# Output and MLP down-projection in weight blocks of 512 rows by 512 columns instead of 1024 by 256

## The chip, the cores and the metric

The kernel runs on one core of one Trainium2 chip. The metric is device time in microseconds of one execution; before the change it is the median of three runs.

## The reference

A two-layer hybrid backbone works on 256 context tokens and 256 latent tokens of width 1024, all in float32. In each layer three parallel mixers read one input projection, their branches are projected and merged by sigmoid gates, and one output projection follows. Then comes a squared-ReLU MLP. Both results are normalised, scaled by a gate and added to the residual stream. In the second layer only the latent tokens are needed.

```python
def merge_branches(ys, gates, w_branch, w_out):
    g = jax.nn.sigmoid(gates.reshape(gates.shape[:2] + (N_BRANCHES, D_MODEL)))
    merged = g[..., 0, :] * (ys[0] @ w_branch[0])
    for j in range(1, N_BRANCHES):
        merged = merged + g[..., j, :] * (ys[j] @ w_branch[j])
    return merged @ w_out

def sq_relu_mlp(h, w_up, w_down):
    return jnp.square(jax.nn.relu(h @ w_up)) @ w_down
...
        x = x + m_l[2] * rms_norm(y_l, norm_g[l, 1])
        h_l = modulate(rms_norm(x, norm_g[l, 2]), m_l[3], m_l[4])
        x = x + m_l[5] * rms_norm(sq_relu_mlp(h_l, w_mlp_up[l], w_mlp_down[l]), norm_g[l, 3])
```

The two products that the change touches are `merged @ w_out` (1024 by 1024) and `... @ w_down` (4096 by 1024).

## The kernel before

**Numbers in two parts.** Every float32 operand of a large product is split into a high part (rounded to the matmul's reduced format) and a low part (what is left). A product is summed from three matmuls: high by high, high by low and low by high. `weights` (L196) loads a block of 128 x 2048 values in two transfers into one of five `raw` slots, then makes the high part by four casts of 128 x 512 on ScalarE (L226) and the low part by four subtractions on VectorE (L227). Two such blocks fit into `whl`, so that one is converted while the other is used. `wblock` (L232) names the rows and columns of the weight that go into a block.

**Two forms of product.** `mm_cm` (L241) holds 128 x 128 of the weight stationary and moves up to 512 tokens; its matmuls are on L248 to L250. `mm_tm` (L252) holds 128 tokens of the activation stationary and moves columns of the weight, so that the result has tokens on the partitions; its matmuls are on L260 to L262. Each result is summed in one of eight PSUM banks of 512 float32 columns. From the output projection on, `dps` deals four of them out in turn, as b_84 to b_87 in the names below.

**The stage of the change.** `tm_out` (L636) computes the output projection and the MLP's down-projection with `mm_tm`. The tokens are four row tiles of 128: 0 and 1 the context, 2 and 3 the latents; layer 1 has only 2 and 3. A block is 1024 rows (eight steps of 128) by 256 columns, so the output's 1024 columns take four blocks. For each block and each row tile 8 x 3 matmuls of 256 columns are summed in half a bank. The tile is then taken out:

```python
if add:
    nc.vector.tensor_tensor(out=o, in0=src, in1=o, op=ALU.add)
    src = o
elif not gains:
    nc.scalar.copy(o, src)
if gains:
    nc.scalar.activation(junk[:, 0:256], src, AF.Square, scale=D ** -0.5, accum_out=yss[tt][:, b:b + 1])
    nc.vector.tensor_tensor(out=o, in0=src, in1=gains(tt)[:, b * 256:b * 256 + 256], op=ALU.mult)
```

The MLP's hidden width of 4096 is done in four quarters (`qd`): an up-projection of 1024 columns (`cm_blocks`), then `tm_out` over these 1024 rows of `w_down`. Quarter 0 copies the sum out (L655), quarters 1 to 3 add to it (L652), and in quarter 3, as in the output projection, the sum of squares (L657) and the multiply by the gain (L659) follow. `seqs` lists which row tiles share which block: in layer 0's quarters 0 to 2 all four tiles share each block; in its quarter 3 and its output projection the blocks are loaded once for tiles 0 and 1 and again for 2 and 3; in layer 1 tiles 2 and 3 share each block, and the last two blocks are held together, so that tile 2 is done before tile 3.

**What follows a finished row tile.** `after` runs `post` (the mean of squares L629, the power -1/2 on GpSimd L454, and the update of the residual L633), then `prenorm` (Square L566, the sum L568, L454, scaling on VectorE L573 and ScalarE L575, eight transposes on TensorE L581) and `modulate` (scale and shift L598 on VectorE and L596 on ScalarE, high part L603, low part L605), which writes the next stage's activations `h`. After the kernel's last product only `post` and the store of the output are left.

**What sets the order.** Each engine executes its instructions in one order that a scheduler fixes at build time from priorities; conversions and what takes tiles out of PSUM have a higher priority (`hp`). In layer 0's MLP VectorE also computes the second layer's modulation vectors (`ada_acc`, L403), a few steps after each weight block.

## Time and profile before

| what | value |
|---|---|
| median of three runs | 1625.68 us (1623.34 to 1628.14) |
| the profiled execution's own time | 1622.66 us |
| its span | 1620.9 us |
| TensorE busy | 1569.2 us (97%) |
| VectorE busy | 1091.5 us (67%) |
| ScalarE busy | 782.5 us (48%) |
| GpSimd busy | 387.8 us (24%) |
| transfers | 220.26 MB, mean 136 GB/s |

The span runs from the first to the last instruction of the profiled execution; the 1.8 us beside it are its start and end. Shares of busy time are means over stages with different limits, and a matmul's busy time overlaps that of the next one, so a stage is read from the starts of its matmuls and from what its engines wait for. PE is TensorE, PEld its weight loads, DVE VectorE, ACT ScalarE, POOL GpSimd and SP the queue of the transfers. L12 is line 12 of the kernel.

### The profile page before, as it was taken

The page shows a single profiled execution, that of the slowest core. Times are in us where ns is not written, and L with a number is a line of the kernel's source. Part 1 is how long each engine was busy: PE and PEld are TensorE (multiplying, and loading weights), DVE is VectorE, ACT ScalarE, POOL GpSimd, SP SyncE. Part 2 cuts the span into 40 slices and gives each one's busy share as a digit, 9 for nine tenths or more (in the row PEclk, how much of TensorE's full clock was granted, in tenths as well). Part 3 has the DMA queues.
Part 4 walks back from the last instruction along what each step waited for, and adds up shares of the span by engine and source line. Part 5 has one row for each costly group of instructions (what it writes and reads, how often), then busy time and mean ns, then how long its engine had stood idle before and what let it go on. Part 6 is the DMA issues. An engine that isn't in the chain of part 4 may idle for free.

```text
span 1620.9 us, 30093 instructions
## 1 busy us (share of the span) xinstructions
PE 1569.2 (97%) x11806; PEld 1401.7 (86%) x11806; DVE 1091.5 (67%) x1994; ACT 782.5 (48%) x1648; POOL 387.8 (24%) x419
## 2 busy tenths in 40 slices
PE   6999999999999999999999999999998999989998
PEld 4788888887777789888898989999897999989998
DVE  4655544676576578687878756776668788765555
ACT  4443433455444457533323146644455656666554
POOL 1142415050510001310102011364455350211001
PEclk9999999999999999999999999999999999989999
DMA  9723243324332346466556534432434254446662
GB/s 282 230 79 118 80 130 117 92 66 130 129 93 53 117 141 195 147 189 188 173 178 195 156 104 133 129 118 73 124 104 105 66 162 113 156 131 182 183 182 92
DMA packets 234270, 220.26 MB, mean 136 GB/s; under 512 B 24400, under 2 KB 226320, under 8 KB 234128
## 3 DMA queue, kind: packets, MB, share of 16 engines
q1 hardware_dynamic: 234128, 218.34, 45.1%
q8 instruction: 92, 1.51, 0.4%
q14 instruction: 50, 0.41, 0.1%
HBM read 217.26 MB, written 1.05 MB: 135 GB/s over the span
## 4 chain that ended last, share of the span: by engine, by line
PE 84%; DVE 4%; POOL 4%; DMA 2%; ACT 2%; issue 2%; SPq 1%; DVEq 0%; POOLq 0%; ACTq 0%
PE b L248 15%; PE b L249 15%; PE b L250 15%; PE b L260 9%; PE b L261 9%; PE b L262 9%; DMA arf<-in_w_ada_dram 1%; POOL arf L906 1%; PE b L364 1%; POOL arf L796 1%; PE b L1109 1%; PE b L936 1%; PE b L1096 1%; DVE whl L227 1%; PE b L937 1%
## 5 line engine op out<-in xcount | busy, mean ns | idle before, releaser
L227 DVE TENSOR_TENSOR whl<-raw,whl 128x512 fp32r<-128x512 f32 x588 | 431.9, 755 | 213.0 <-ACT whl L226 201.0
L226 ACT CAST whl<-raw 128x512 fp32r<-128x512 f32 x588 | 356.1, 619 | 247.5 <-PE b L262 111.8
L248 PE MATMUL b<-h,whl 128*128 128x512 f32 (+1 forms) x1296 | 448.1, 347 | 1.1 <-ACT arf L951 0.6
L250 PE MATMUL b<-h,whl 128*128 128x512 f32 (+1 forms) x1296 | 445.4, 344 | 0.9 <-DVE whl L227 0.8
L249 PE MATMUL b<-h,whl 128*128 128x512 f32 (+1 forms) x1296 | 444.7, 343 | 0.0
L248 PEld LDWEIGHTS b<-h,whl 128*128 128x128 f32 x1296 | 247.7, 191 | 33.4 <-ACT whl L226 2.1
L250 PEld LDWEIGHTS b<-h,whl 128*128 128x128 f32 x1296 | 246.8, 191 | 29.4 <-issue 1.6
L249 PEld LDWEIGHTS b<-h,whl 128*128 128x128 f32 x1296 | 247.1, 191 | 28.1 <-issue 2.4
L262 PE MATMUL b<-whl,arr 128*128 128x256 f32 x768 | 215.9, 284 | 1.9 <-DVE arr L1320 1.9
L261 PE MATMUL b<-whl,arr 128*128 128x256 f32 x768 | 217.5, 284 | 0.0
L260 PE MATMUL b<-whl,arr 128*128 128x256 f32 x768 | 217.5, 284 | 0.0
L1319 POOL TENSOR_TENSOR arf<-arf 128x256 f32<-128x256 f32 (+1 forms) x68 | 62.3, 916 | 427.7 <-ACT arr L1318 424.1
L260 PEld LDWEIGHTS b<-whl,arr 128*128 128x128 f32 x768 | 147.5, 192 | 1.4 <-DVE arf L652 0.8
L262 PEld LDWEIGHTS b<-whl,arr 128*128 128x128 f32 x768 | 146.8, 192 | 2.1 <-DVE arr L1320 2.1
L261 PEld LDWEIGHTS b<-whl,arr 128*128 128x128 f32 x768 | 147.5, 192 | 0.1
L260 PE MATMUL b<-whl,h 128*128 128x256 f32 x512 | 146.6, 288 | 0.0
L261 PE MATMUL b<-whl,h 128*128 128x256 f32 x512 | 146.0, 286 | 0.0
L262 PE MATMUL b<-whl,h 128*128 128x256 f32 x512 | 144.7, 285 | 0.0
L906 POOL TENSOR_TENSOR arf<-arf,cst 32x256 f32<-32x256 f32 x104 | 94.3, 907 | 192.7 <-ACT arf L951 71.0
L454 POOL TENSOR_TENSOR sm<-sm,nhalf 128x1 f32<-128x1 f32 (+2 forms) x42 | 33.2, 794 | 345.2 <-DVE sm L629 247.2
L403 DVE SCALAR_TENSOR_TENSOR arf<-arf,CA 128x1024 f32<-128x1024 f32 x84 | 109.3, 1345 | 4.8 <-DMA arf<-in_w_ada_dram 4.8
L260 PEld LDWEIGHTS b<-whl,h 128*128 128x128 f32 x512 | 98.6, 193 | 3.2 <-ACT arf L740 0.8
(224 smaller groups left out, 2504.3 us busy)
## 6 DMA issues: line engine op xcount, KB each, us to landing
raw<-in_w_in_dram SPq DMA_DIRECT2D x110, 512.0 KB, 3.9
arf<-in_w_ada_dram SPq DMA_DIRECT2D x80, 512.0 KB, 4.7
raw<-in_w_mlp_down_dram SPq DMA_DIRECT2D x72, 512.0 KB, 3.7
raw<-in_w_mlp_up_dram SPq DMA_DIRECT2D x64, 512.0 KB, 3.9
raw<-in_w_out_dram SPq DMA_DIRECT2D x24, 512.0 KB, 3.6
arf<-in_w_ada_dram SPq DMA_DIRECT2D x32, 256.0 KB, 5.8
raw<-in_w_branch_dram SPq DMA_DIRECT2D x16, 512.0 KB, 4.2
raw<-in_w_in_dram SPq DMA_DIRECT2D x32, 128.0 KB, 3.3
```

Of the source, the lines that this page charges most:

```text
L226: self.behind(ops, lambda: nc.scalar.copy(r32(h), src))
L227: self.split_op = self.behind(ops, lambda: nc.vector.tensor_tensor(out=r32(l), in0=src, in1=h, op=ALU.subtract))
L248: nc.tensor.matmul(ps, wh, xh[:, t0:t0 + n], start=start and k == 0, stop=False)
L249: nc.tensor.matmul(ps, wh, xl[:, t0:t0 + n], start=False, stop=False)
L250: nc.tensor.matmul(ps, wl, xh[:, t0:t0 + n], start=False, stop=stop and k == nk - 1)
L260: nc.tensor.matmul(ps, xh, wh, start=start and k == 0, stop=False)
L261: nc.tensor.matmul(ps, xh, wl, start=False, stop=False)
L262: nc.tensor.matmul(ps, xl, wh, start=False, stop=stop and k == nk - 1)
L403: self.nc.vector.scalar_tensor_tensor(out=a[:, :], in0=raw[:, :], scalar=ca[:, k, s:s + 1], in1=a[:, :], op0=ALU.mult, op1=ALU.add)
L454: self.nc.gpsimd.tensor_tensor(out=r, in0=ms, in1=self.nhalf[:, 0:cols], op=ALU.pow)
L906: nc.gpsimd.tensor_tensor(out=b[o, 0:LAT], in0=x[i], in1=self.cst[i, C_RS:C_RS + LAT], op=ALU.mult)
L1319: nc.gpsimd.tensor_tensor(out=r[:, c], in0=r[:, c], in1=r[:, c], op=ALU.mult)
```

## The change

A block is now 512 rows (four steps of 128) by 512 columns: the same 2048 columns in `whl`, the same bytes. An output column half takes two blocks, one for the upper and one for the lower 512 rows (`kh` 0 and 1), and a row tile's sum over both fills a whole PSUM bank. `order` takes all row tiles of a group through `kh` 0, each into a bank of its own, then all through `kh` 1, and takes each tile out when its second part is done. In layer 1's last group (`whole`) both blocks are loaded first, and tile 2 is finished before tile 3. The operations that take a tile out work on 512 columns instead of 256, and a row tile has two partial sums of squares instead of four.

```diff
--- before.py
+++ after.py
@@ -135,7 +135,7 @@
         self.oml = const("oml", 8)
         self.nhalf = const("nhalf", 8)
         self.ones = const("ones", 32)
-        self.yss = const("yss", 20)
+        self.yss = const("yss", 12)
         self.sm_t = const("sm", 512)
         self.sm_i = 0
         self.raw = const("raw", RAWS * 1024)
@@ -638,26 +638,38 @@
 
         nc = self.nc
         junk = self.A.get(1)
-        left = {tt: 4 for tt in y}
-        for tts, blocks in seqs:
-            blks = [(b, self.wblock(w, r0, 8, b * 256, 256)) for b in blocks]
-            for tt in tts:
-                for b, blk in blks:
-                    ps = self.dps()
-                    self.mm_tm(ps[:, 0:256], blk, 8, 0, 256, act, tt)
-                    o = y[tt][:, b * 256:b * 256 + 256]
-                    with self.hp():
-                        src = ps[:, 0:256]
-                        if add:
-                            nc.vector.tensor_tensor(out=o, in0=src, in1=o, op=ALU.add)
-                            src = o
-                        elif not gains:
-                            nc.scalar.copy(o, src)
-                        if gains:
-                            nc.scalar.activation(junk[:, 0:256], src, AF.Square, scale=D ** -0.5,
-                                                 accum_out=yss[tt][:, b:b + 1])
-                            nc.vector.tensor_tensor(out=o, in0=src, in1=gains(tt)[:, b * 256:b * 256 + 256], op=ALU.mult)
-                left[tt] -= len(blks)
+        left = {tt: 2 for tt in y}
+
+        def finish(tt, b, ps):
+            o = y[tt][:, b * 512:b * 512 + 512]
+            with self.hp():
+                src = ps
+                if add:
+                    nc.vector.tensor_tensor(out=o, in0=src, in1=o, op=ALU.add)
+                    src = o
+                elif not gains:
+                    nc.scalar.copy(o, src)
+                if gains:
+                    nc.scalar.activation(junk[:, :], src, AF.Square, scale=D ** -0.5, accum_out=yss[tt][:, b:b + 1])
+                    nc.vector.tensor_tensor(out=o, in0=src, in1=gains(tt)[:, b * 512:b * 512 + 512], op=ALU.mult)
+            left[tt] -= 1
+
+        for tts, halves, whole in seqs:
+            for b in halves:
+                ps = {}
+                order = [(kh, tt) for kh in range(2) for tt in tts]
+                blks = {}
+                if whole:
+                    order = [(kh, tt) for tt in tts for kh in range(2)]
+                    blks = {kh: self.wblock(w, r0 + kh * 512, 4, b * 512, 512) for kh in range(2)}
+                for kh, tt in order:
+                    if kh not in blks:
+                        blks[kh] = self.wblock(w, r0 + kh * 512, 4, b * 512, 512)
+                    if not kh:
+                        ps[tt] = self.dps()
+                    self.mm_tm(ps[tt], blks[kh], 4, 0, 512, act, tt, kt0=kh * 4, start=not kh, stop=kh == 1)
+                    if kh:
+                        finish(tt, b, ps[tt])
             for tt in tts:
                 if gains and left[tt] == 0:
                     after(tt)
@@ -1273,10 +1285,10 @@
         sv = self.scale_vecs(l, 1)
         y = {tt: A.get(2) for tt in tts}
         if not last:
-            seqs = [((0, 1), (b,)) for b in range(4)] + [((2, 3), (b,)) for b in range(4)]
+            seqs = [((0, 1), (0, 1), False), ((2, 3), (0, 1), False)]
         else:
-            seqs = [((2, 3), (0,)), ((2, 3), (1,)), ((2, 3), (2, 3))]
-        yss = {tt: self.yss[:, tt * 5:tt * 5 + 5] for tt in tts}
+            seqs = [((2, 3), (0,), False), ((2, 3), (1,), True)]
+        yss = {tt: self.yss[:, tt * 3:tt * 3 + 3] for tt in tts}
 
         late = []
 
@@ -1355,11 +1367,11 @@
                 if not last:
                     sv = self.scale_vecs(l + 1, 0)
             if last and qd == 3:
-                seqs = [((2, 3), (0,)), ((2, 3), (1,)), ((2, 3), (2, 3))]
+                seqs = [((2, 3), (0,), False), ((2, 3), (1,), True)]
             elif qd == 3:
-                seqs = [((0, 1), (b,)) for b in range(4)] + [((2, 3), (b,)) for b in range(4)]
+                seqs = [((0, 1), (0, 1), False), ((2, 3), (0, 1), False)]
             else:
-                seqs = [(tts, (b,)) for b in range(4)]
+                seqs = [(tts, (0, 1), False)]
             self.tm_out(I["w_mlp_down"][l], qd * 1024, act, y, yss, seqs, qd > 0, gains if qd == 3 else None, after)
             for b in ab.values():
                 b.free()
```

TensorE at the start of quarter 0's down-projection in layer 0 (b_85 and b_86 are the banks of row tiles 0 and 1, `arr` holds the activations, `whl` the weights). Before, tile 1's steps with a jump back to tile 0's last step:

```order
L262 MATMUL b_86<-whl,arr 128x256
L260 MATMUL b_86<-whl,arr 128x256
L261 MATMUL b_86<-whl,arr 128x256
L260 MATMUL b_85<-whl,arr 128x256
L261 MATMUL b_85<-whl,arr 128x256
L262 MATMUL b_86<-whl,arr 128x256
```

After, the same place at the step from tile 0 to tile 1:

```order
L260 MATMUL b_85<-whl,arr 128x512
L261 MATMUL b_85<-whl,arr 128x512
L262 MATMUL b_85<-whl,arr 128x512
L260 MATMUL b_86<-whl,arr 128x512
L261 MATMUL b_86<-whl,arr 128x512
```

Before, the schedule leaves tile 0 after 21 of its 24 matmuls, ahead of the step on the eighth activation, and comes back to it; now a tile's run is twelve matmuls on four activations, and the eighth activation is used only after all four tiles have had their first run.

VectorE at the end of layer 1's output projection (b_86 is tile 3's last result, b_88 to b_91 the transposed rows, `sm` and `yss` the sums). Before:

```order
L629 TENSOR_REDUCE sm<-yss 128x1
L659 TENSOR_TENSOR arf<-b_86,arf 128x256
L573 TENSOR_SCALAR arf<-arf,sm 128x512
L633 SCALAR_TENSOR_TENSOR arf<-arf,sm 128x512 x2
L598 TENSOR_SCALAR arf<-b_90,sb,M_67 128x128 x3
L598 TENSOR_SCALAR arf<-b_89,sb,M_67 128x128 x3
L568 TENSOR_SCALAR sm<-sm 128x1
L605 TENSOR_TENSOR h<-arf,h 128x4x128
L573 TENSOR_SCALAR arf<-arf,sm 128x512
L598 TENSOR_SCALAR arf<-b_91,sb,M_67 128x128 x4
L603 CAST h<-arf 128x4x128
L605 TENSOR_TENSOR h<-arf,h 128x4x128 x2
```

After (the multiply of L659 is now on L654):

```order
L629 TENSOR_REDUCE sm<-yss 128x1
L654 TENSOR_TENSOR arf<-b_86,arf 128x512
L633 SCALAR_TENSOR_TENSOR arf<-arf,sm 128x512 x2
L568 TENSOR_SCALAR sm<-sm 128x1 x2
L573 TENSOR_SCALAR arf<-arf,sm 128x512 x2
L598 TENSOR_SCALAR arf<-b_89,sb,M_67 128x128 x3
L598 TENSOR_SCALAR arf<-b_90,sb,M_67 128x128 x3
L598 TENSOR_SCALAR arf<-b_91,sb,M_67 128x128 x4
L603 CAST h<-arf 128x4x128
L605 TENSOR_TENSOR h<-arf,h 128x4x128 x3
```

Tile 2's six L598 and its L605 stood ahead of tile 3's L573; now both tiles' L568 and L573 stand ahead of all ten L598, and three L605 stand at the end.

VectorE at the end of the kernel (b_85 and b_86 were tile 3's last two results, b_86 is now its last). Before:

```order
L652 TENSOR_TENSOR arf<-b_85,arf 128x256
L659 TENSOR_TENSOR arf<-arf 128x256
L652 TENSOR_TENSOR arf<-b_86,arf 128x256
L629 TENSOR_REDUCE sm<-yss 128x1
L659 TENSOR_TENSOR arf<-arf 128x256
L633 SCALAR_TENSOR_TENSOR arf<-arf,sm 128x512 x2
```

After (the add of L652 is now on L648):

```order
L633 SCALAR_TENSOR_TENSOR arf<-arf,sm 128x512 x2
L648 TENSOR_TENSOR arf<-b_86,arf 128x512
L629 TENSOR_REDUCE sm<-yss 128x1
L654 TENSOR_TENSOR arf<-arf 128x512
L633 SCALAR_TENSOR_TENSOR arf<-arf,sm 128x512 x2
```

The order of the last steps is the same; the add and the multiply of the last tile are twice as wide, and there is one pair of them where there were two.

## Rows read from the trace of the kernel before

**Rows 1.** The page: span, TensorE's busy time (PEld its weight loads), chain that ended last.
```profile
span 1620.9 us, 30093 instructions
...
PE 1569.2 (97%) x11806; PEld 1401.7 (86%) x11806; DVE 1091.5 (67%) x1994; ACT 782.5 (48%) x1648; POOL 387.8 (24%) x419
...
PE 84%; DVE 4%; POOL 4%; DMA 2%; ACT 2%; issue 2%; SPq 1%; DVEq 0%; POOLq 0%; ACTq 0%
```

**Rows 2.** Stretches: length, then busy us per engine, granted clock, DMA share, GB/s.
```profile
620.00:640.00 20.00, 20.00 (x171) 20.00 (x170) 18.74 (x42) 18.14 (x47) 4.25 (x6) 1.00 0.62 189
1000.00:1040.00 40.00, 40.00 (x337) 40.00 (x337) 36.45 (x79) 29.71 (x74) 12.96 (x13) 1.00 0.61 181
1440.00:1600.00 160.00, 160.00 (x1336) 160.00 (x1335) 88.80 (x158) 90.98 (x180) 18.12 (x30) 1.00 0.56 170
1422.00:1432.00 10.00, 8.19 (x35) 7.17 (x36) 7.92 (x19) 8.00 (x17) 1.82 (x2) 0.50 0.03 5
```

**Rows 3.** Timeline of TensorE, last down-projection: start us, duration us, line, tiles.
```profile
1599.72 0.28 PE L262 MATMUL b<-whl,arr 128*128 128x256 f32 x1
...
1612.20 0.28 PE L261 MATMUL b<-whl,arr 128*128 128x256 f32 x1
```

**Rows 4.** Timeline of TensorE, a branch projection of layer 0.
```profile
299.65 0.39 PE L248 MATMUL b<-arr,whl 128*128 128x512 f32 x1
...
306.00 0.39 PE L249 MATMUL b<-arr,whl 128*128 128x512 f32 x1
```

**Rows 5.** Groups by line and shape, TensorE: xcount, busy us, mean ns, idle before.
```profile
L261 PE MATMUL b<-whl,arr 128*128 128x256 f32 x768 | 217.5, 284 | 0.0
...
L249 PE MATMUL b<-h,whl 128*128 128x256 f32 x608 | 173.7, 286 | 0.0
...
L260 PE MATMUL b<-whl,h 128*128 128x256 f32 x512 | 146.6, 288 | 0.0
```

**Rows 6.** Waits of TensorE: us in total, times, longest.
```profile
PE b L262 <- DVE arr L1320: 1.9, 1, 1.9
...
PE b L248 <- ACT h L603: 1.5, 1, 1.5
...
PE b L249 <- POOL h L605: 0.7, 1, 0.7
```

**Rows 7.** Groups by line and shape: conversions (L227, L226), eviction L652, multiply L1167.
```profile
L227 DVE TENSOR_TENSOR whl<-raw,whl 128x512 fp32r<-128x512 f32 x588 | 431.9, 755 | 213.0 <-ACT whl L226 201.0 <-PE b L250 3.6 <-PE b L249 2.5
L226 ACT CAST whl<-raw 128x512 fp32r<-128x512 f32 x588 | 356.1, 619 | 247.5 <-PE b L262 111.8 <-PE b L249 82.9 <-issue 13.7
...
L652 DVE TENSOR_TENSOR arf<-b,arf 128x256 f32<-128x256 f32 x72 | 30.0, 422 | 29.3 <-PE b L262 27.9
...
L1167 DVE TENSOR_TENSOR arf<-b,arf 128x512 f32<-128x512 f32 x24 | 16.5, 690 | 20.6 <-PE b L250 20.5
```

**Rows 8.** Timeline, layer 1, end of the output projection to the MLP's first matmul.
```profile
1421.05 2.00 DVE L598 TENSOR_SCALAR arf<-b,sb,M 128x128 f32<-128x128 f32 x6
...
1423.96 0.48 DVE L573 TENSOR_SCALAR arf<-arf,sm 128x512 f32<-128x512 f32 x1
...
1425.73 1.37 DVE L598 TENSOR_SCALAR arf<-b,sb,M 128x128 f32<-128x128 f32 x4 [1.30 <-PE b L581]
...
1427.62 0.79 PE L248 MATMUL b<-h,arr 128*128 128x256 f32 x2 [1.07 <-DVE h L603]
```

**Rows 9.** Timeline, after the kernel's last matmul.
```profile
1614.44 0.42 DVE L652 TENSOR_TENSOR arf<-b,arf 128x256 f32<-128x256 f32 x1 [0.73 <-PE b L262]
1614.96 0.42 ACT L657 ACTIVATE arf<-arf 128x256 f32<-128x256 f32 x1 [1.71 <-DVE arf L652]
...
1615.74 0.66 POOL L454 TENSOR_TENSOR sm<-sm,nhalf 128x1 f32<-128x1 f32 x1 [4.87 <-DVE sm L629]
```

**Rows 10.** Transfers: count, KB each, median us from issue to landing.
```profile
raw<-in_w_mlp_down_dram SPq DMA_DIRECT2D x72, 512.0 KB, 3.7
...
raw<-in_w_branch_dram SPq DMA_DIRECT2D x16, 512.0 KB, 4.2
```

## The prediction

> **What bounds the kernel now.** I read the page first. TensorE is busy for 1569.2 of the 1620.9 us span, and the chain of work that ended last lies on it for 84% [rows 1]. Busy time of pipelined matmuls says little about their pace, so I next cut the span into stretches: in layer 0's output projection (620 to 640), in its last down-projection (1000 to 1040) and through layer 1's MLP (1440 to 1600) TensorE is never idle and its granted clock is full, 2.4 GHz; VectorE is behind it at 18.74 of 20, 36.45 of 40 and 88.80 of 160 us [rows 2]. So in the stages that the change touches the pace of matmuls sets the time, and that is what to price. Third came the timeline of TensorE for that pace, and last the list of its waits and the two places where they sum up.
>
> **The pace.** In a down-projection the 256-column matmul at 1599.72 and the 104th after it, at 1612.20, are 12.48 us apart: 0.1200 us from start to start [rows 3]. In a branch projection 512-column matmuls go from 299.65 to 306.00 in 28 steps: 0.2268 us [rows 4]. Two of the former take 0.2400 us, one of the latter 0.2268, for the same columns: 13.2 ns per pair is paid once less.
>
> **The change, part by part.**
>
> (a) Matmuls. The down-projections issue 768 matmuls on each of the three lines [rows 5]. The row for the 512 on `h` also holds other projections; from the code the output projection has 4 x 4 x 8 = 128 of them in layer 0 and 2 x 4 x 8 = 64 in layer 1. So (768 + 192) x 3 = 2880 matmuls of 256 columns become 1440 of 512: 2880 x 0.1200 = 345.6 us becomes 1440 x 0.2268 = 326.6 us. All of it lies on the path, as TensorE does not idle there: **-19.0 us**.
>
> (b) Row block order. In quarter 0 of layer 0 TensorE waits once, 1.9 us, for the low part of the last activation from VectorE (L262 on L1320) [rows 6], because the first tiles need all eight activations at once. Now the first four tiles use only activations 0 to 3, and that is 4 x 12 x 0.2268 = 10.9 us of matmuls before activation 4 is wanted. The wait goes: **-1.9 us**, end 0 if something else is late there.
>
> (c) Conversions and evictions. The same 48 weight blocks are loaded and converted, four casts of 619 ns and four subtractions of 755 ns each [rows 7]. A tile's two 256-column evictions of 422 ns become one of 512; the nearest such operation, a multiply out of PSUM, takes 690 ns [rows 7]. Where two row tiles share a block, VectorE's need per block was 4 x 0.755 + 4 x 0.42 = 4.7 of 5.76 us, and becomes 4 x 0.755 + 2 x 0.69 = 4.4 of 5.44 us: 82% and 81%. So I cost conversions at nothing; their cover is TensorE's own work on the block before. What is not even is the order. In layer 0's output projection the two chains to the next layer norm share VectorE and ScalarE with conversions, and these are fullest there (18.74 and 18.14 of 20 us [rows 2]); TensorE already waits 1.5 + 0.7 us behind it for the modulated `h` [rows 6]. A longer chain (Square and eviction of 512) or a late conversion adds to that. The ends are -2.2 (the waits vanish) and +3.0 (as much again and a conversion); I take **+1.0 us**, near the waits there now.
>
> (d) Layer 1's output projection into the MLP. Here nothing covers the layer norm. Today VectorE does six L598 of the first tile in 2.00 us from 1421.05, while the second tile's norm is still under way; L573 of the second follows at 1423.96, its four L598 at 1425.73, and TensorE starts at 1427.62 [rows 8]. In the new order both L573 stand ahead of all ten L598 on VectorE, so the 2.00 us no longer lie beside the wait but behind it, and a third L605 stands behind them. Ends: 0.2 (only the Square grows) and 2.8 (2.0 and one subtraction of 0.755 more [rows 7]); I take **+1.5 us**, nearer to the full 2.0. TensorE is at half its clock (1.2 GHz) for 10 us after that idle time today [rows 2], and stays so for as long, so that adds nothing.
>
> (e) The end. After the last matmul come eviction, Square, mean, L454 and the last update. The eviction grows from 0.42 to 0.69 us, the Square from 0.42 [rows 9] to some 0.62 (the cast of 512 elements on ScalarE [rows 7]); the gain multiply lies beside L454's 0.66 us [rows 9]. **+0.5 us**.
>
> (f) Transfers. Their number and bytes stay; the pieces of a row grow from 256 to 512 columns. Blocks of that shape exist in the branch projection and land in 4.2 us, the down-projection's in 3.7 [rows 10]. Up to 0.5 us later with five slots ahead: nothing, as no wait of TensorE on these blocks is in the list. The step from layer 0 to layer 1 has a whole first block pair on the first two tiles as cover: nothing, end 0.5.
>
> **Sum:** -19.0 - 1.9 + 1.0 + 1.5 + 0.5 = -17.9 us. On the profiled execution's own 1622.66 us this gives 1604.8. The median of the runs shown is 1625.68, 3.0 above it, which would give 1607.8; I forecast **1606**, between the two.
>
> **A rule against it.** The rows give a matmul 13.3 ns beyond its columns at either width: 0.1200 against 256 / 2.4 GHz = 0.1067, 0.2268 against 0.2133 [rows 3, 4]. The Trainium skill, TensorE: Matmul & The Clock Gate, section Back-to-back issue gap, puts the fixed part of a warm matmul at 2.5 ns for one isolated gap; by that the pair would save 2.5 ns, 3.6 us in all, and the sum would give 1620.2. The trace disagrees with that figure at both widths, so the measurement decides.
>
> **The rivals.**
>
> 1. *Little or no saving per pair.* The 512-column rows are of the other form (weights stationary, activations moving). Should the form with moving weights run at twice its 256-column pace, 0.2400, term (a) is nothing and the rest leaves 1622.66 + 1.1 = 1623.8 us, the same. For it: no row has this form at 512 columns. Against it: at 256 columns the two forms last alike, 284 and 286 ns [rows 5], and rows 3 and 4 give both widths the same extra time. That the change does not happen is excluded, since the compiled order has the 128x512 tiles. Chance 0.04, and the page's saving of 2.5 ns is within it.
>
> 2. *VectorE becomes the bound in layer 0's two-tile stages.* Its shares are 94% (620 to 640) and 91% (1000 to 1040) [rows 2]. If TensorE can't go faster there, the 192 pairs of layer 0's output projection and 192 of its last quarter save nothing: 384 x 0.0132 = 5.1 us back, 1609.9 on the profiled execution's count, 1611 on mine. For it: shares above 90%. Against: VectorE's need shrinks as fast as TensorE's. Chance 0.08.
>
> 3. *Slower: each hand-over of a two-tile block shows one piece's conversion.* A block half now serves two tiles of 2.72 us, and the buffer's first piece is free only when the second tile has passed it, 8.2 us before it is needed again (8.6 today). If VectorE and ScalarE come more than 8.2 - 0.62 - 4 x 0.755 = 4.5 us late, one cast and subtraction, 1.37 us, is open at each of 36 such blocks (12 in output projections, 8 and 16 in down-projections): 49 us, so 1655. It decides against the kernel from 0.5 us per block on (17.9 / 36). For it: 18.74 of 20 us. Against: the list of TensorE's waits has none of L260 to L262 on L226 or L227, and in layer 1 VectorE has 71 of 160 us free [rows 2]. Chance 0.04.
>
> **Numbers.** 0.3% of 1622.66 is 4.9 us, about what a measurement can tell here. Forecast 0.84, rival 2 0.08 (both faster), rivals 1 and 3 0.04 each: faster 0.92, same 0.04, slower 0.04. The ends of (b) to (f) move the sum from -22.4 (c at -2.2, d at 0.2) to -12.2 (b at 0, c at 3.0, d at 2.8, f at 0.5; e in both): 1600.3 to 1610.5 on the profiled count, 3.0 more on the median's. With rival 2 inside, the range is **1599 to 1615**.
>
> **What would show it.** Right: L260 to L262 with 128x512 tiles, 0.227 us from start to start, no idle TensorE in the down-projections; L262's wait on L1320 gone; TensorE's restart in layer 1 a microsecond or two later after the last L262 than today. Wrong: a pace near 0.24 (rival 1); TensorE idle on L226 or L227 in layer 0's two-tile stages (rival 2) or at block borders everywhere (rival 3). The forecast itself would be wrong if the granted clock fell in the runs of 512-column matmuls; the pace of rows 4 is that of the full clock, which speaks against it.

## The result, and the profile after

The changed kernel takes 1607.04 us (median of four runs, 1605.77 to 1608.23) where the kernel before took 1624.72 beside it: a ratio of 0.9888, with a 95% interval of 0.9869 to 0.9907, or 17.7 us less. The forecast was 1606, the range 1599 to 1615. The profiled execution took 1608.23 us, its span 1606.5, 14.4 less than the span before.

The page of the changed kernel: TensorE has 1440 instructions fewer and is busy 18.3 us less, VectorE 6.2 us less; the chain that ended last lies on TensorE as before [rows 1].

```profile
span 1606.5 us, 27064 instructions
...
PE 1550.9 (97%) x10366; PEld 1325.8 (83%) x10366; DVE 1085.3 (68%) x1934; ACT 776.5 (48%) x1588; POOL 393.2 (24%) x419
...
PE 86%; DVE 5%; POOL 4%; DMA 2%; issue 1%; ACT 1%; SPq 1%; POOLq 0%; DVEq 0%; ACTq 0%
```

The groups by line and shape (count, busy us, mean ns of one, idle before): the down-projections' 768 matmuls per line [rows 5] are 384 of 512 columns, with no idle time ahead of them; the add on L648 (L652 before) lasts 688 ns for 512 columns, the 0.69 that the prediction took.

```profile
L260 PE MATMUL b<-whl,arr 128*128 128x512 f32 x384 | 149.9, 392 | 0.0
...
L648 DVE TENSOR_TENSOR arf<-b,arf 128x512 f32<-128x512 f32 x36 | 24.8, 688 | 19.1 <-PE b L262 19.0
```

The timeline of TensorE, layer 1's last down-projection: 96 matmuls, from 1576.40 to 1597.96 in 95 steps, 0.2269 us from start to start, the pace of rows 4.

```profile
1576.40 0.40 PE L260 MATMUL b<-whl,arr 128*128 128x512 f32 x1
...
1597.96 0.39 PE L262 MATMUL b<-whl,arr 128*128 128x512 f32 x1
```

TensorE's waits (us in total, times, longest): the wait of L262 on VectorE's low part is gone; the one for `h` in layer 0's hand-over (1.5 in rows 6) is 3.4, and one of 5.0 in layer 1's hand-over stands where the kernel before has three shorter ones (1.2, 2.2 and 1.1).

```profile
PE b L581 <- DVE arf L573: 5.0, 1, 5.0
...
PE b L248 <- ACT h L603: 3.4, 1, 3.4
```

From such starts of matmuls the span can be cut at each first and last matmul on L260 to L262. This gives the lengths of the table (us); "again" is another profiled execution of the same kernel, from the experiments. A stage counts from its first to its last start, a gap from the last start to the next stage's first; so a gap holds the last matmul, which is 0.11 us longer now. The gap into layer 1 ends at the first group of layer 1's mixers on `whl`. The spans are given to 0.1 us, so the last row is good to 0.05.

| stretch | before | again | after | again | again |
|---|---|---|---|---|---|
| start to layer 0's output projection | 590.72 | 591.03 | 592.78 | 592.14 | 591.37 |
| its output projection | 56.18 | 56.18 | 53.49 | 53.50 | 53.50 |
| hand-over into the MLP and first up-projection | 50.91 | 51.09 | 52.05 | 52.19 | 53.11 |
| down-projection, quarter 0 | 49.69 | 49.72 | 45.05 | 45.05 | 45.05 |
| quarters 1 and 2, each | 47.57 | 47.57 | 45.05 | 45.05 | 45.05 |
| quarter 3 | 47.76 | 47.75 | 45.29 | 45.29 | 45.28 |
| gap into layer 1 | 42.66 | 42.66 | 43.75 | 43.80 | 43.79 |
| layer 1's mixers, stretch A | 59.97 | 60.00 | 61.01 | 60.97 | 60.16 |
| layer 1's mixers, stretch B | 68.49 | 68.52 | 69.07 | 69.02 | 68.57 |
| layer 1's output projection | 26.10 | 26.10 | 24.54 | 24.44 | 24.44 |
| hand-over into the MLP and first up-projection | 35.08 | 35.07 | 34.15 | 34.14 | 34.14 |
| each of its four down-projections | 22.92 | 22.92 | 21.56 | 21.56 | 21.56 |
| last matmul's start to the end | 6.78 | 6.79 | 8.54 | 8.47 | 8.51 |

Stretch A runs from the end of the second to the start of the third group of L260 to L262 in layer 1's mixers, B from there to the end of the fourth. Every stage with the new blocks is shorter, in each profile by the same amount within 0.1 us. Four stretches between them are longer, and one is shorter.

### The profile page after: what moved, and what is told of

The parts are those of the page before. It is cut to its first block, busy times and chain, and to the rows that moved or that the text cites. A ratio compares the mean times of both kernels' runs of the same rounds, so it can differ in the third digit from the quotient of the medians.

```text
span 1606.5 us, 27064 instructions
## 1 busy us (share of the span) xinstructions
PE 1550.9 (97%) x10366; PEld 1325.8 (83%) x10366; DVE 1085.3 (68%) x1934; ACT 776.5 (48%) x1588; POOL 393.2 (24%) x419
## 4 chain that ended last, share of the span: by engine, by line
PE 86%; DVE 5%; POOL 4%; DMA 2%; issue 1%; ACT 1%; SPq 1%; POOLq 0%; DVEq 0%; ACTq 0%
PE b L248 16%; PE b L249 16%; PE b L250 16%; PE b L260 9%; PE b L261 9%; PE b L262 9%; POOL arf L918 2%; PE b L364 1%; PE b L1121 1%; PE b L1108 1%; PE b L868 1%; PE b L948 1%; DVE whl L227 1%; PE b L949 1%; PE b L852 1%
## 5 line engine op out<-in xcount | busy, mean ns | idle before, releaser
L227 DVE TENSOR_TENSOR whl<-raw,whl 128x512 fp32r<-128x512 f32 x588 | 429.9, 751 | 215.6 <-ACT whl L226 206.4
L226 ACT CAST whl<-raw 128x512 fp32r<-128x512 f32 x588 | 356.0, 620 | 260.2 <-PE b L262 114.8
L248 PE MATMUL b<-h,whl 128*128 128x512 f32 (+1 forms) x1296 | 448.2, 348 | 1.2 <-ACT arf L963 0.6
L248 PEld LDWEIGHTS b<-h,whl 128*128 128x128 f32 x1296 | 248.2, 192 | 33.8 <-ACT whl L226 2.1
L260 PE MATMUL b<-whl,arr 128*128 128x512 f32 x384 | 149.9, 392 | 0.0
L262 PE MATMUL b<-whl,arr 128*128 128x512 f32 x384 | 149.9, 390 | 0.0
L261 PE MATMUL b<-whl,arr 128*128 128x512 f32 x384 | 149.7, 390 | 0.0
L260 PE MATMUL b<-whl,h 128*128 128x256 f32 (+1 forms) x416 | 129.5, 314 | 0.0
L261 PE MATMUL b<-whl,h 128*128 128x256 f32 (+1 forms) x416 | 129.0, 311 | 0.0
L262 PE MATMUL b<-whl,h 128*128 128x256 f32 (+1 forms) x416 | 128.7, 311 | 0.0
L454 POOL TENSOR_TENSOR sm<-sm,nhalf 128x1 f32<-128x1 f32 (+2 forms) x42 | 34.5, 826 | 332.7 <-DVE sm L629 242.8
L808 POOL TENSOR_TENSOR arf<-arf 128x512 f32<-128x512 f32 x56 | 75.8, 1374 | 46.1 <-ACT arf L787 32.6
L260 PEld LDWEIGHTS b<-whl,h 128*128 128x128 f32 x416 | 80.2, 193 | 6.5 <-issue 0.8
L260 PEld LDWEIGHTS b<-whl,arr 128*128 128x128 f32 x384 | 72.1, 188 | 15.9 <-issue 1.2
L262 PEld LDWEIGHTS b<-whl,arr 128*128 128x128 f32 x384 | 72.1, 188 | 15.0
```

What stands on the lines that cost most here:

```text
L226: self.behind(ops, lambda: nc.scalar.copy(r32(h), src))
L227: self.split_op = self.behind(ops, lambda: nc.vector.tensor_tensor(out=r32(l), in0=src, in1=h, op=ALU.subtract))
L248: nc.tensor.matmul(ps, wh, xh[:, t0:t0 + n], start=start and k == 0, stop=False)
L260: nc.tensor.matmul(ps, xh, wh, start=start and k == 0, stop=False)
L261: nc.tensor.matmul(ps, xh, wl, start=False, stop=False)
L262: nc.tensor.matmul(ps, xl, wh, start=False, stop=stop and k == nk - 1)
```

## The experiments

Times are medians; ratios are to the kernel before, run beside each.

**The changed kernel again.** The same program, twice.

> The changed kernel once more, unaltered. It measures what an execution moves by itself: the changed kernel's profile lost 2.0 us before layer 0's output projection and 1.6 us within layer 1's mixers against the profile of before, in stages whose order of instructions is the same. Theory: that is scatter, and it comes out differently here, with the time again near 1607 us and 1.1% below before. Rival: the change shifts something in those stages (an address, a transfer) and the same 2.0 and 1.6 us are lost again.

Measured: 1607.55 us, ratio 0.9891 (0.9876 to 0.9906). All stages repeat within 0.15 us, but the first 590 us, which the change does not touch, are 0.6 us shorter. Much later:

> The changed kernel, unchanged, beside the next run on the same chip. Expected at 1607 to 1607.5, with every stage's length as in its first two profiles within 0.15 us, layer 1's mixers at 61.0 and 69.05 us among them. Rival (the extra 1.6 us in these mixers come and go from one execution to the next): 60.0 and 68.5.

Measured: 1606.22 us, 0.9889 (0.9869 to 0.9908). Here the rival holds: stretch A is 60.16 and B 68.57, within 0.2 us the lengths of the kernel before, while layer 0's hand-over is 1.06 longer. So these three differ from one execution to the next; the gap into layer 1, layer 1's hand-over and the end do not in these three profiles.

**The kernel before again.**

> The kernel before, unchanged, profiled once more. Theory (where TensorE waits for a microsecond or two, the granted clock falls behind the wait in some executions and not, or not as long, in others, so that lengths of stages with waits differ from run to run though nothing in them changed): layer 0's hand-over into the MLP (50.9 us) and two stretches of layer 1's mixers (60.0 and 68.5 us) come out at one of two lengths, about 49.4 or 50.9, 60.0 or 61.0, 68.5 or 69.1, while the stages without waits repeat within 0.05 us. Rival (the differences come with the change): all of these repeat at 50.9, 60.0 and 68.5 within 0.1 us.

Measured: 1623.27 us. All the stretches named repeat within 0.2 us, nearly as the rival has it. This alone would have put 1.6 us of the mixers down to the change; the run above shows that the changed kernel has both lengths. In the twelve profiles of this document with new blocks in either place, stretch A is 60.87 to 61.17 us in nine and 60.09 to 60.16 in three. Whether the change makes the longer one more frequent stays open, as there are two profiles of the kernel before. One repeat that agrees is not enough for a stretch with waits.

What differs is seen in stretch A. The windows of the changed kernel's first profile (length, busy us of PE, PEld, DVE, ACT, POOL, granted clock, DMA share, GB/s), 12.6 us after the stretch begins:

```profile
1138.00:1140.00 2.00, 0.70 (x19) 0.69 (x20) 2.00 (x3) 0.40 (x1) 2.00 (x2) 1.00 0.21 75
1140.00:1142.00 2.00, 0.48 (x9) 0.31 (x11) 2.00 (x4) 0.00 (x0) 1.52 (x2) 0.77 0.13 17
1142.00:1144.00 2.00, 1.89 (x37) 1.65 (x38) 2.00 (x8) 0.77 (x2) 0.00 (x0) 0.50 0.80 253
1144.00:1146.00 2.00, 2.00 (x11) 2.00 (x11) 0.69 (x1) 0.92 (x2) 0.00 (x0) 0.50 0.00 0
1146.00:1148.00 2.00, 2.00 (x12) 2.00 (x12) 1.07 (x2) 0.93 (x2) 0.00 (x0) 0.52 0.00 0
```

The same view of its last profile, 13.0 us after the stretch begins:

```profile
1138.00:1140.00 2.00, 1.06 (x19) 1.03 (x20) 2.00 (x3) 0.40 (x1) 2.00 (x3) 0.69 0.05 17
1140.00:1142.00 2.00, 1.17 (x20) 0.79 (x19) 2.00 (x6) 0.00 (x0) 1.16 (x1) 0.50 0.23 37
1142.00:1144.00 2.00, 1.89 (x25) 1.76 (x23) 1.64 (x7) 0.77 (x2) 0.00 (x0) 0.50 0.72 234
1144.00:1146.00 2.00, 2.00 (x13) 2.00 (x12) 0.71 (x2) 1.24 (x2) 0.00 (x0) 0.61 0.00 0
1146.00:1148.00 2.00, 2.00 (x20) 2.00 (x19) 1.79 (x4) 1.59 (x5) 0.48 (x2) 1.00 0.05 6
```

The instructions are the same. TensorE is mostly idle at first, and the granted clock falls from 1.00 to 0.50 (2.4 to 1.2 GHz), in the last profile sooner, in the first later. So it also comes back later there, and dense matmuls that run at full pace in the last profile run at half pace in the first (20 and 12 in the last window).

**What a matmul costs.** In layer 1's down-projections every 512-column matmul is issued as two.

```diff
-ps[tt] = self.dps()
+ps[tt] = [self.dps(), self.dps()]
...
-self.mm_tm(ps[tt], blks[kh], 4, 0, 512, act, tt, kt0=kh * 4, start=not kh, stop=kh == 1)
+for c in range(2):
+    self.mm_tm(ps[tt][c][:, 0:256], blks[kh], 4, c * 256, 256, act, tt, kt0=kh * 4, start=not kh, stop=kh == 1)
```

> The changed kernel, but in layer 1's four down-projections every 512-column matmul is issued as two of 256 columns into two PSUM banks, each taken out in its own 256-column pieces. Blocks of 512 x 512, their transfers and conversions and the order of row blocks stay. Theory (a part of the time of a matmul does not depend on its columns, 13.2 ns per pair): each of these four stages has 96 pairs and goes from 21.56 us (first to last matmul start) back to 22.92, so 4 x 1.27 = +5.1 us against the changed kernel, about 1612.5. Rival A (the saving comes from the new blocks and their order, from transfers of longer rows or from fewer evictions): the stages stay at 21.56 and the time at about 1607.5. Rival B (two banks per tile leave TensorE waiting for evictions): the stages get longer than 22.92.

Measured: all four stages are 22.92 us long, those of the kernel before to the hundredth, with the new blocks, transfers and row-block order in place. The timeline of its last one, 192 matmuls in 191 steps of 0.1200 us:

```profile
1577.49 0.28 PE L260 MATMUL b<-whl,arr 128*128 128x256 f32 x1
...
1600.41 0.28 PE L262 MATMUL b<-whl,arr 128*128 128x256 f32 x1
```

This version also doubles the evictions, which the next run shows to take no part. So the saving in these stages is the pace of matmuls alone; rivals A and B fall. Each split matmul has a weight load of its own (10750 of each on this profile's page), so the runs do not tell whether the 13.2 ns belong to the matmul or to that load. For the other stages there is no such run: the version that splits all 1440 gave no time. The time is 1610.18 us (0.9908, 0.9893 to 0.9923), 2.3 less than expected, 1.75 of it as its end is 6.79 us instead of 8.54: with 256-column halves the first half is taken out beside the second.

**Evictions in halves.** 512-column matmuls, but every tile is taken out in two pieces of 256 columns.

```diff
-src = ps
+for c in (0, 256):
+    src = ps[:, c:c + 256]
```

> The changed kernel with 512-column matmuls, but every finished tile is taken out in two halves of 256 columns with the operations of before (two adds, two Squares, two multiplies). Theory (only matmuls count, VectorE and ScalarE are covered): 1607 us within 1.5, the end after the last matmul within 0.5 us of the changed kernel's 8.5. Rival (VectorE's 8.8 us and ScalarE's some 10 us saved by the wider operations carry a part of the gain): 1610 us or more, with TensorE waiting in layer 0's output projection or last quarter.

Measured: 1613.03 us, 0.9923 (0.9908 to 0.9938). The stages stay at 45.05 and 21.56, so evictions take no part in their length. But the theory's 1607 is missed by 6 us: the time is the rival's, though not for its reason, as TensorE does not wait in the stages that it names. The time is lost between them: layer 0's hand-over is 53.49, the gap into layer 1 44.48, and layer 1's hand-over 39.79 instead of 34.15. There the compiled order takes the two tiles' transposes apart again, eight, then the broadcasts, then eight; TensorE waits four times, starts the MLP 13.66 us after its last L262 (10.46 in the changed kernel), and its clock is down for 16 us:

```profile
1411.00:1427.00 16.00, 12.18 (x51) 10.42 (x52) 13.85 (x29) 11.23 (x25) 2.89 (x4) 0.50 0.22 65
```

**Tile 3 behind tile 2, in both of layer 1's last groups.**

```diff
-self.mm_tm(ps[tt], blks[kh], ...)
+with self.tc.issue_after(self.tm_op.ins) if whole and tt == tts[1] and not kh else nullcontext():
+    self.mm_tm(ps[tt], blks[kh], ...)
```

> The changed kernel with one constraint more: in the last group of layer 1's two projections the first matmul of tile 3 comes after the last of tile 2, as the code is written; without it the schedule puts nine matmuls of tile 3 ahead of the end of tile 2. Theory (tile 2 ends 2.0 us too late, so that its residual update, 1.4 us on VectorE, stands ahead of tile 3's eviction): from the start of the last matmul to the end of the span 8.5 us becomes 7.3 (before: 6.8, and 0.5 for the wider add and Square), so about 1.2 us less time. Rival (the end is longer because its operations are wider, or because of the store): it stays at 8.5 us.

Measured: 1611.29 us, 0.9918 (0.9901 to 0.9935), slower than the changed kernel. The end is 7.62 us, 0.9 shorter, not quite the 7.3 expected. But layer 1's output projection is 26.88 instead of 24.54, mostly since TensorE now waits for the second block's conversion, which tile 3's interleaved matmuls had covered, and its hand-over 35.70 instead of 34.15:

```profile
1398.73 0.50 PE L260 MATMUL b<-whl,h 128*128 128x512 f32 x1 [1.00 <-ACT whl L226]
1399.65 0.50 PE L261 MATMUL b<-whl,h 128*128 128x512 f32 x1 [0.41 <-DVE whl L227]
```

**The same in the last down-projection alone** (`whole and add` in the condition).

> The changed kernel, but in the very last block group (layer 1's last down-projection) tile 3's first matmul is issued after tile 2's last one. Theory (the end grew by 1.8 us mostly because the compiled order puts nine of tile 3's matmuls among tile 2's, so that tile 2's update stands in front of tile 3's eviction on VectorE): from the last matmul's start to the end of the span 8.5 us become about 7.6, as in the run with this constraint in both stages, and nothing else changes, as the conversions there are long done: about 1606.5. Rival (the end grew by the wider operations alone): it stays at 8.5 and the time at 1607.5.

Measured: 1606.19 us, 0.9883 (0.9867 to 0.9898); the end is 7.62 us and every other stretch within 0.15 us of what the changed kernel's own profiles show. The theory holds; this order makes half of the longer end. Tile 3's add now waits for the last matmul and no longer for tile 2's update:

```profile
1598.60 0.69 DVE L648 TENSOR_TENSOR arf<-b,arf 128x512 f32<-128x512 f32 x1 [1.06 <-PE b L262]
```

**The rest of the end.** The last group is also cut into two column halves, one after the other.

```diff
+for j in range(2):
+    pc = self.dps()[:, 0:256]
+    for h in range(2):
+        self.mm_tm(pc, blks[h], 4, j * 256, 256, act, tt, kt0=h * 4, start=not h, stop=h == 1)
+    finish(tt, b, pc, j * 256, 256, j)
```

> The changed kernel with tile 3's last group behind tile 2's last matmul (as in the run before with that alone), and that last group issued as two column halves of 256 one after the other, each summed over all eight steps in a bank of its own and taken out by itself. Theory (what is left of the longer end are the wider eviction and Square, and they need be wide only where TensorE's pace is won): the first half is taken out beside the second half's 24 matmuls, so the end from the last matmul's start goes from 8.5 us to about 6.8 as before the change, for 12 pairs x 13.2 ns = 0.16 us more of matmuls: 1.5 to 1.6 us less than the changed kernel, about 1605.5 to 1606. Rival (VectorE's order decides, tile 2's update still stands ahead): the end stays at 7.6 or longer, 1606.5.

> The version with the last group behind tile 2 and issued as two column halves, once more beside the changed kernel. Theory (its end is 1.77 us shorter, its last group 0.4 longer, nothing else differs): 1.3 to 1.4 us under the changed kernel, about 1605.8. Rival (another stage gives it back): within 0.5 us of the changed kernel.

Measured: 1605.70 us (0.9884, 0.9869 to 0.9899), and again 1604.88 (0.9877, 0.9861 to 0.9893) beside 1606.22 of the changed kernel. The end is 6.77 and 6.78 us, the last down-projection 21.98 (+0.42), so 1.35 us are won in these two stretches in both profiles. Not all else is alike: in the second profile layer 1's output projection is 25.09 and the hand-over behind it 34.53. The whole time agrees with that, but its intervals overlap those of the changed kernel: the gain is shown by the stretches, not by the ratio.

**TensorE kept busy in layer 1's hand-over.**

```diff
+if whole and not add:
+    d = self.dps()
+    for _ in range(44):
+        nc.tensor.transpose(d[:, 0:128], self.ident, self.ident)
```

> The changed kernel, but in layer 1's hand-over from the output projection to the MLP TensorE runs 44 transposes of a constant (about 4.8 us at full clock) into a PSUM bank that nobody reads, right behind the last matmul of the output projection, where it stands idle for 5.0 us now. Theory (the length of this hand-over depends on when the granted clock falls and comes back: it falls to 0.50 behind the idle time and the 16 transposes and 8 broadcasts behind it run at half pace, 3.47 + 1.6 us): with TensorE busy the clock stays at 1.00, the transposes take 1.7 us, and the first up-projection matmul comes 1 to 2 us earlier, so 1 to 2 us off the 34.1 us from the last to the first matmul of the neighbouring stages; time about 1606. Rival (the hand-over is set by VectorE's and ScalarE's chain, and TensorE's pace hides beside it): the first up-projection matmul starts at most 0.3 us earlier and the time stays at 1607.5; if the extra transposes last over 5.0 us they push the real ones back, and it is slower by that.

Measured: 1607.24 us, 0.9890 (0.9873 to 0.9907). The clock does stay at 1.00 through the transposes, and the 16 of L581 and the first broadcasts begin to wait for the other engines:

```profile
1406.73 4.96 PE L677 MATMUL b<-cst 128*128 128x128 f32 x44
1412.19 2.02 PE L581 MATMUL b<-cst,arf 128*128 128x128 f32 x16 [0.49 <-DVE arf L573]
1414.62 0.65 PE L619 MATMUL b<-cst,sm 128*128 128x128 f32 x4 [0.42 <-ACT arf L596]
1416.86 0.47 PE L248 MATMUL b<-h,arr 128*128 128x256 f32 x2 [1.58 <-ACT arf L596]
```

The first L248 comes 10.36 us after the last L262, in the changed kernel 10.46: the rival holds, the hand-over's length up to there is VectorE's and ScalarE's. And the idle time behind the transposes now brings the clock down where work is dense, as the windows show, so the stretch becomes 36.39 us, 2.2 longer:

```profile
1415.00:1417.00 2.00, 0.41 (x4) 0.20 (x3) 1.93 (x6) 2.00 (x6) 0.45 (x1) 1.00 0.00 0
1417.00:1419.00 2.00, 1.22 (x10) 1.01 (x11) 2.00 (x3) 2.00 (x5) 0.85 (x1) 1.00 0.00 0
1419.00:1421.00 2.00, 2.00 (x13) 2.00 (x12) 2.00 (x4) 2.00 (x5) 0.00 (x0) 0.53 0.03 8
1421.00:1423.00 2.00, 2.00 (x13) 2.00 (x13) 2.00 (x4) 1.01 (x2) 0.00 (x0) 0.61 0.48 114
```

**One half of the change at a time.** The old `tm_out` is kept under another name and used in one of the two places.

> New blocks in the down-projections alone; the output projections as before. Theory (costs add up by stage): the output projections go back to 56.2 and 26.1 us (+2.7 and +1.6 against the changed kernel), the down-projections keep the new lengths (45.05 and 21.56 us), and the hand-overs into the MLP go back to 50.9 and 35.1 us (-1.1 and +0.9): about +4, so 1611.5. Rival (the new blocks in the output projection cost as much in the hand-overs as they save, as with the smaller evictions): within 1 us of the changed kernel, 1607.5.

Measured: 1609.12 us, 0.9904 (0.9886 to 0.9922): 2 us above the changed kernel, between theory and rival, which the intervals do not part. The down-projections have all their new lengths, quarter 0's 45.05 among them. Layer 0's hand-over is 49.36, 1.5 under the kernel before with the same order of work: its windows show a granted clock of 1.00 throughout, where those of the kernel before have 0.55 from 664 to 666 and 0.60 from 666 to 668. So this one profile says less about the output projection than the stages do. Layer 1's hand-over does not go back to 35.1 either: it is 33.41, shorter than in both kernels, though TensorE does the same in the same order as in the kernel before and starts the MLP as long after its last L262, 9.74 us. Its granted clock is back at 1.00 when the MLP begins (windows, and the first L248 of the timeline):

```profile
1411.00:1413.00 2.00, 1.75 (x9) 1.35 (x10) 1.42 (x4) 1.97 (x4) 0.99 (x2) 0.57 0.00 0
1413.00:1415.00 2.00, 1.71 (x8) 1.30 (x7) 1.11 (x4) 0.30 (x2) 0.83 (x1) 0.58 0.00 0
1415.00:1417.00 2.00, 0.91 (x5) 0.73 (x6) 1.39 (x4) 1.97 (x6) 0.00 (x0) 1.00 0.00 0
...
1415.77 0.50 PE L248 MATMUL b<-h,arr 128*128 128x256 f32 x2 [1.07 <-DVE h L603]
```

> New blocks in the output projections alone; the down-projections as before. Theory (costs add up by stage): output projections 53.5 and 24.5 us, layer 0's hand-over about 1.0 us longer than before at equal granted clock (up to 1.7 us more or less where the clock falls otherwise), layer 1's about 0.9 shorter, all down-projections at their old 49.7, 47.6 and 22.9 us, the end at 6.8: 2 to 5 us under the kernel before, 1621 to 1623. Rival (the output projections' saving is given back in the hand-overs): within 1 us of the kernel before.

Measured: 1619.53 us, 0.9968 (0.9956 to 0.9979), 3.4 to 7.1 us under the kernel before: the theory holds in the difference, 4.8, though not in the level, which is 1.5 us below its 1621. The output projections are 53.49 and 24.44, layer 0's hand-over 53.31, layer 1's 34.14, the end 6.72. The gap into layer 1 is 42.65, so its growth belongs to the down-projection's new blocks. Quarter 0, with old blocks, is 47.57: the wait of L262 is gone here as well, where the hand-over ahead of it is 2.4 us longer.

## Why the prediction was right, step by step

The differences of the first pair of profiles, with the 0.11 us of the wider last matmul moved from each gap into its stage, against the terms of the sum:

| term | predicted | measured |
|---|---|---|
| (a) pace of matmuls | -19.0 | -18.6 |
| (b) wait in quarter 0 | -1.9 | -2.1 |
| (c) layer 0's hand-over into the MLP | +1.0 | +1.0 |
| (d) layer 1's hand-over | +1.5 | -1.0 |
| (e) the end | +0.5 | +1.65 |
| (f) gap into layer 1 | 0 | +1.0 |
| mixers of layer 1 | not in the sum | +1.7 |
| start to the first output projection | not in the sum | +2.1 |
| other gaps | 0 | -0.1 |
| sum | -17.9 | -14.4 |

The two stretches outside the sum change from one execution of the same kernel to the next (the mixers by 1.4 us between profiles of the changed kernel, the start by 1.4). Over several runs the medians differ by 17.7 us, next to the predicted sum of 17.9. So close a match is luck: (d) came out 2.5 us lower than taken, (e) and (f) together 2.15 higher, and these errors largely cancelled. What was right for its reason is (a), which is the bulk of the saving.

(a) was right for the reason given. The run with split matmuls puts back 1.36 us per down-projection (96 pairs, one shorter last matmul of 0.11 included) and nothing else of its stages, so 13.2 ns per pair are paid for each matmul more, at either width and in this form too; for the other stages this is carried over from their equal lengths per pair. Rival 1 falls. The Trainium skill, TensorE: Matmul & The Clock Gate, section Back-to-back issue gap, puts the fixed part of a warm matmul at 2.5 ns for an isolated gap. Rows 3 and 4 show 13.3 ns, and the new profiles repeat it, so the measurement decides. Rivals 2 and 3 fall with layer 0's stages: its two-tile stages lost 2.69 and 2.47 us for 192 pairs, about as much as the four-tile quarters 1 and 2 (2.52), and the changed kernel's list of waits has none of L260 to L262 on L226 or L227.

(b) was right in size. That the row-block order suffices is shown by the version with new blocks in the down-projections alone, where the wait is gone after a shorter hand-over. A longer hand-over takes it away as well.

(c) was right in size in the first pair: the wait on L603 went from 1.5 to 3.4 us, while the 0.7 on L605 is gone. Whether the wider operations or a late conversion make the wait longer was not tried. In the last execution of the same kernel the wait is the same and the length 1.1 more: behind the wait the granted clock is below 1.00 in four windows of 2 us (0.72, 0.50, 0.50, 0.57) instead of three (0.80, 0.50, 0.84).

(d) failed. Its first half was right in kind: both L573 stand ahead of all ten L598, and the first L248 comes 10.46 us after the last L262 instead of 9.74, half of what was taken. TensorE now waits once and runs all 16 transposes (L581) and 8 broadcasts (L619) in one piece. The timelines before and after:

```profile
1417.88 0.28 PE L262 MATMUL b<-whl,h 128*128 128x256 f32 x1
1419.39 1.09 PE L581 MATMUL b<-cst,arf 128*128 128x128 f32 x8 [1.23 <-ACT arf L575]
1422.72 2.12 PE L619 MATMUL b<-cst,sm 128*128 128x128 f32 x8 [2.24 <-ACT arf L596]
1424.63 1.92 PE L581 MATMUL b<-cst,arf 128*128 128x128 f32 x8
...
1407.79 0.39 PE L262 MATMUL b<-whl,h 128*128 128x512 f32 x1
1413.16 3.68 PE L581 MATMUL b<-cst,arf 128*128 128x128 f32 x16 [4.98 <-DVE arf L573]
1416.63 1.50 PE L619 MATMUL b<-cst,sm 128*128 128x128 f32 x8
1418.25 0.50 PE L248 MATMUL b<-h,arr 128*128 128x256 f32 x2
```

The step that failed is "stays so for as long, so that adds nothing". From the first L248 to the first down-projection it is 25.34 us before and 23.69 after. In the windows of the changed kernel the clock falls sooner and is back before the MLP begins, where the kernel before was at 0.50 from 1422 to 1432, 4.4 us into the MLP [rows 2, 8]:

```profile
1411.00:1413.00 2.00, 0.00 (x0) 0.00 (x0) 1.34 (x5) 1.89 (x5) 0.76 (x2) 0.50 0.15 58
1413.00:1415.00 2.00, 1.84 (x9) 1.84 (x10) 1.27 (x5) 0.94 (x2) 0.51 (x1) 0.50 0.00 0
1415.00:1417.00 2.00, 2.00 (x11) 2.00 (x10) 2.00 (x8) 1.51 (x4) 0.36 (x1) 0.50 0.00 0
1417.00:1419.00 2.00, 1.63 (x10) 1.18 (x8) 1.93 (x5) 2.00 (x6) 0.91 (x1) 0.86 0.00 0
1419.00:1421.00 2.00, 1.93 (x16) 1.96 (x17) 2.00 (x4) 2.00 (x5) 0.00 (x0) 1.00 0.00 0
```

That the new order brings the clock back sooner is not shown. The version with new blocks in the down-projections alone has the old order and the same 9.74 us, and there too the clock is back before the MLP begins; its 33.41 us are 1.7 under the kernel before. Against that profile the new order costs 0.7 us, with the sign that was predicted. The new order gave 34.13 to 34.53 in all eight profiles that have it without extra transposes, the old one 35.08, 35.07 and 33.41. Whether the order makes the early return more frequent stays open.

(e) was mis-sized. The wider add and Square cost 0.25 and 0.21 us, the 0.5 that was taken. Not seen was where tile 2 ends. The compiled order does not finish tile 2 before tile 3: it puts nine of tile 3's matmuls among tile 2's, so tile 2 ends 15 matmuls before the end, and its update L633 stands in front of tile 3's last add. The text ahead of the prediction calls the order of the last steps the same, but its rows of the order after begin with this L633; before, it stood ahead of the last add but one. The last matmul of the kernel before, and the timeline of VectorE and GpSimd in the changed kernel:

```profile
1614.12 0.28 PE L262 MATMUL b<-whl,arr 128*128 128x256 f32 x1
...
1597.36 0.55 POOL L454 TENSOR_TENSOR sm<-sm,nhalf 128x1 f32<-128x1 f32 x1 [18.84 <-DVE sm L629]
1597.94 1.41 DVE L633 SCALAR_TENSOR_TENSOR arf<-arf,sm 128x512 f32<-128x512 f32 x2 [0.66 <-POOL sm L454]
...
1599.28 0.68 DVE L648 TENSOR_TENSOR arf<-b,arf 128x512 f32<-128x512 f32 x1
...
1600.88 0.68 DVE L654 TENSOR_TENSOR arf<-arf 128x512 f32<-128x512 f32 x1
1601.04 0.93 POOL L454 TENSOR_TENSOR sm<-sm,nhalf 128x1 f32<-128x1 f32 x1 [3.13 <-DVE sm L629]
```

The add comes 1.32 us after the last matmul's start at 1597.96; before it was 0.32 (1614.12, and 1614.44 in rows 9). That is 1.0 us, 0.11 of it the longer last matmul; the last 0.27 is L454, 0.93 instead of 0.66, which the prediction kept at 0.66. The two runs on the end undo it: tile 3 behind tile 2 gives 0.9 back, column halves the rest.

(f) was wrong by 1.0 us, which repeats in every version with new blocks in quarter 3 of layer 0 and is absent without them. The step that failed is the cover: it was taken that a whole block pair on the first two tiles hides the hand-over. The changed kernel's first profile has two waits of TensorE there, 0.31 us for `h` (L605) and 0.33 for a copy out of PSUM (L752), where the kernel before has one of 0.23. They make some 0.4 of the 1.0 us; the cause of the rest, and of the waits, stays open.

## What to carry to other kernels

Where TensorE never idles, price a tiling by the measured start-to-start time of each shape: it held here to some 0.2 us per stage, and was not moved by blocks, evictions or transfers. Then look at each place where the engine does wait, and read the compiled order there line by line: of the three terms that were wrong, one was a step that came to stand in front of another, and one hung on where a half-clock stretch fell, which differs between profiles that have the same order. Before a microsecond of a single pair of profiles is explained, profile the same kernel more than once.

## What was not expected of the hardware

The granted clock fell behind waits such as the 5.0 us in layer 1's hand-over and the 3.4 us in layer 0's, and the same instructions then take one of two or more lengths: 61.01, 60.97 and 60.16 us for one stretch of one program. Behind the waits of 1.5 and 0.7 us in layer 0's hand-over it fell in the kernel before and stayed at 1.00 in the version with new blocks in the down-projections alone. Keeping TensorE busy through one idle time did not save the fall; in that version it fell 12.6 us after the last L262 instead of 2.9 (worked out from the windows' means), at a worse place.

GpSimd's power of one column (L454) lasted 0.93 us while VectorE's multiply beside it was 512 columns wide, and 0.66 beside one of 256 (rows 9, and the version with column halves). With no multiply beside it, it lasted 0.55 (at 1597.36), and in the changed kernel it ends 0.41 us after the multiply does, as in the version with column halves: as if it went on only behind the multiply. What the two share was not tried.
